# Decays of a delta rule: masked products and matmuls, or a row of running sums and a biased exp

## The chip, the cores and the metric

The program runs on 1 core of one Trainium2 chip. The core has a matrix engine (PE, with its weight loads PEld), a vector engine (DVE), a scalar engine (ACT), GpSimd (POOL) and DMA queues that its SyncE (SP), ACT and POOL issue to. The metric is the device time of one execution in microseconds, lower is better. Each engine runs its own instructions in a fixed order; an instruction that waits holds up all that stand behind it on the same engine or queue.

## The reference, cut to what matters

One residual layer over 1024 tokens of 1024 channels: a projection, two branches (a gated delta rule with 8 heads, and gated linear attention with 4), their output projections, gates and a norm. Both branches run forward and backward. The change touches the delta rule alone. For one head and one direction, within a chunk:

```python
g = jnp.cumsum(to_chunks(g), axis=-1)              # running sums of log decays
diff = g[..., :, None] - g[..., None, :]
decay = jnp.where(incl, jnp.exp(jnp.where(incl, diff, 0.0)), 0.0)
kb = k * beta[..., None]
lower = jnp.where(strict, jnp.einsum("bhnid,bhnjd->bhnij", kb, k) * decay, 0.0)
sol = lax.linalg.triangular_solve(lower, rhs, left_side=True, lower=True, unit_diagonal=True)
attn = jnp.einsum("bhnid,bhnjd->bhnij", q, k) * decay
v_new = u_n - w_n @ S
o = qd_n @ S + attn_n @ v_new
S = S * exp(gl_n) + kd_n^T @ v_new
```

The keys k are normalised to length one. The kernel works in chunks of 128 tokens, which gives the same result.

## The kernel before

The tokens lie in 8 chunks of 128. Channels are on the partitions, tokens on the free axis, except for keys and values by tokens (`ktok`, `vtok`). The program has these stages in order: the norm of x and its transposes; the gates of the scans (`scan_gates`, L407); eight heads of the delta rule; four heads of linear attention; two output projections; the merged output.

For each head h of the delta rule there are four pieces. `gdn_project` (L487) projects the keys, queries and values (`pj_a`) and the gate z (`pj_z`), convolves them on DVE (L506, L508) and applies SiLU on ACT (L489). `gdn_decay` (L573) makes `dt`, the decay from token j to token i for 16 units (8 chunks by 2 directions). `gdn_inverse` (L592) takes the norms of the keys (L608, into `n2`), the products of the keys (`pgr`, L624), multiplies them by `dt` and a factor c1 (beta over the squared norm) into `um` (L629), and inverts 1 + um: copies into `ul` on ACT (L636), blocks of 32 by substitution on DVE (L652, L654, 480 instructions each in all), blocks of 64 and 128 by matmuls (L683 to L722). Last it multiplies `dt` by the products of keys and queries (L741). `gdn_scan` (L744) runs over the chunks in 8 steps, both directions side by side: `psc` (L779) from the state, `r` on DVE (L781), `psc` (L784) with the inverse, `vd` on DVE (L787) and `vn` on ACT (L789), `psc` (L794) and the new state `S` on DVE (L799), and products into the output `po` (L768).

A scheduler orders each engine's instructions by places that the code gives: the inverse of head h comes first, then the decays of head h + 1 (`P_DT`), then the scan of head h (`P_Z`), which therefore lies beside the next head's inverse. Projections of the next head and, in the last head, 13 blocks of gates (`pj_t`) have the last place (`P_FILL`); their matmuls fill PE wherever nothing else is ready. The order is fixed when the program is built. `dt` has two buffers, so the decays of head h + 1 wait for the end of head h - 1's scan. The banks of `pacc` (tags o0, o1) serve `pd`, the matmuls of the decays, and `po` in turn.

Weights come through SP's queue into two raw buffers (`raw_a` and the like, L174), are cast on ACT into a high part (L177), and get their low part from POOL (L181) or DVE (L183). The row `qe` (L749) is a broadcast of one row of `eg_d` in DRAM to 128 partitions, on SP's queue.

Of the kernel before, what the change touches and what calls it, by code (L numbers as in the profile page):

```python
# [88 lines left out]
def layer_kernel(  # L89
# [200 lines left out]
    # ------------------------------------------------------------ constants of the two mixers  # L290
# [13 lines left out]
    strict_r = [mconst.tile([P, P], F32R, name=f"strict{d}") for d in range(2)]  # L304
    strict = [t.bitcast(F32) for t in strict_r]
# [14 lines left out]
    # ------------------------------------------------------------ h = rmsnorm(x), transposed  # L320
    with tc.tile_pool(name="xpool", bufs=2) as xpool:
        xt = [xpool.tile([P, D], F32, tag="xt", name=f"xt{t}", bufs=NT) for t in range(NT)]
        wpre = xpool.tile([P, D], F32, tag="wpre", name="wpre", bufs=1)
        stl = xpool.tile([P, 2, P], F32, tag="stl", name="stl", bufs=1)
# [20 lines left out]
        def scaled(t):  # L345
            """a tile of x normalised, its transpose"""
# [27 lines left out]
        nc.sync.dma_start(stl, consts[:, CONSTS["su"][0]:CONSTS["su"][0] + 2 * P].rearrange("p (d i) -> p d i", d=2))  # L374
# [9 lines left out]
        for d in range(2):  # L384
            nc.gpsimd.tensor_copy(strict_r[d], stl[:, d])
# [14 lines left out]
    # ------------------------------------------------------------ decays and gates of the scans  # L400
# [753 lines left out]
```

## Time and profile before

| what | value |
|---|---|
| time, median of 3 runs | 1592.54 us (1591.32 to 1592.92) |
| profiled execution: its span, the only time that the page gives of it | 1591.5 us |
| PE busy | 1526.6 us, 96% |
| PEld busy | 1283.3 us, 81% |
| DVE busy | 928.0 us, 58% |
| ACT busy | 673.1 us, 42% |
| POOL busy | 201.8 us, 13% |
| mean granted clock of PE, as a share of 2.4 GHz | 0.982 |

Busy time is the union of an engine's instructions. Matmuls overlap, so PE can be busy all the time and still not issue as fast as it can. The first products of the keys (L624) of the eight heads stand at 87.8, 172.4, 268.1, 357.2, 440.8, 531.4, 611.7 and 703.5 us, and the last scan ends at 797 us; from there to 900 us PE has the gate blocks that are left.

### The profile page before, as it was taken

The numbers are of one execution on the slowest core, as the hardware profiler recorded it, in microseconds if no ns is written. First come the engines' busy times: TensorE is split into PE (matmuls) and PEld (weight loads), VectorE is DVE, ScalarE is ACT, GpSimd is POOL, SyncE is SP. The second block draws the span as 40 slices with busy tenths as digits, with TensorE's granted clock in tenths as the row PEclk, the third lists the DMA queues.
The fourth block names the chain that finished last, engine by engine and source line by source line (L and its number), as shares of the span: only waits on it lengthen the run. The fifth ranks groups of instructions, "written<-read, shape, count | busy, mean of one in ns | idle before, by whom it ended". The sixth has DMA issues, their size and how long they took to land.

```text
span 1591.5 us, 25255 instructions
## 1 busy us (share of the span) xinstructions
PE 1526.6 (96%) x9622; PEld 1283.3 (81%) x9622; DVE 928.0 (58%) x2467; ACT 673.1 (42%) x1370; POOL 201.8 (13%) x225
## 2 busy tenths in 40 slices
PE   6998999999999999999999999999999999999998
PEld 6877787787878878787778898898888988787887
DVE  5497779979999899887511113314323355445413
ACT  5552535343444545453232325525436355433311
POOL 4242112111112121000000120110100100000000
PEclk9998999999999999998999999999999999999999
DMA  5221102121212121024143331231221335655404
GB/s 168 72 73 34 41 28 86 41 73 35 93 34 71 51 81 47 30 81 133 40 142 94 86 75 38 62 79 34 75 59 41 106 89 190 212 169 175 134 27 157
DMA packets 140882, 133.48 MB, mean 84 GB/s; under 512 B 11147, under 2 KB 114875, under 8 KB 140757
## 3 DMA queue, kind: packets, MB, share of 16 engines
q1 hardware_dynamic: 133282, 117.78, 25.0%
q10 hardware_dynamic: 6840, 12.00, 2.5%
q0 software_dynamic: 640, 2.10, 0.4%
q8 instruction: 75, 1.23, 0.3%
q14 instruction: 45, 0.37, 0.1%
HBM read 101.45 MB, written 30.39 MB: 83 GB/s over the span
## 4 chain that ended last, share of the span: by engine, by line
PE 62%; DVE 11%; DMA 6%; ACT 3%; issue 1%; SPq 1%; ACTq 0%; DVEq 0%
PE pj_t L251 9%; PE pj_y L251 7%; PE pj_v L240 6%; PE pout L141 5%; PE pj_a L251 5%; PE pj_g L251 5%; DVE tmp L652 3%; PE pj_q L251 3%; PE pj_k L251 3%; DVE yl L654 3%; PE pj_z L251 2%; PE po L768 2%; PE psb L946 2%; PE pob L968 2%; PE psc L794 1%; DMA st<-ob_d 1%
## 5 line engine op out<-in xcount | busy, mean ns | idle before, releaser
L251 PE MATMUL pj_a<-hh,hi_a 128*128 128x512 f32 x368 | 151.7, 412 | 0.0
L251 PE MATMUL pj_a<-hl,hi_a 128*128 128x512 f32 x368 | 151.0, 410 | 0.0
L251 PE MATMUL pj_a<-hh,lo_a 128*128 128x512 f32 x368 | 150.5, 409 | 0.0
L251 PE MATMUL pj_t<-hh,hi_t 128*128 128x512 f32 x256 | 103.9, 406 | 2.4 <-ACT gt L281 2.4
L251 PE MATMUL pj_t<-hh,lo_t 128*128 128x512 f32 x256 | 104.4, 408 | 0.0
L251 PE MATMUL pj_t<-hl,hi_t 128*128 128x512 f32 x256 | 104.3, 407 | 0.0
L181 POOL TENSOR_TENSOR lo_a<-raw_a,hi_a 128x512 fp32r<-128x512 f32 x48 | 68.6, 1430 | 235.1 <-ACT hi_a L177 224.9
L789 ACT ACTIVATE vn<-psc,c 128x128 f32<-128x128 f32 x128 | 45.0, 366 | 116.4 <-DVE vd L787 88.8
L652 DVE TENSOR_TENSOR tmp<-ulb,yl 128x54 f32<-128x54 f32 (+13 forms) x480 | 93.3, 235 | 1.3 <-DMA yl<-in_consts_dram 1.2
L654 DVE TENSOR_TENSOR yl<-yl,tmp 128x54 f32<-128x54 f32 (+13 forms) x480 | 90.9, 231 | 0.1
L251 PEld LDWEIGHTS pj_a<-hl,hi_a 128*128 128x128 f32 x368 | 71.1, 193 | 12.6 <-issue 1.0
L251 PEld LDWEIGHTS pj_a<-hh,lo_a 128*128 128x128 f32 x368 | 70.6, 192 | 12.8 <-issue 0.7
L251 PEld LDWEIGHTS pj_a<-hh,hi_a 128*128 128x128 f32 x368 | 70.6, 192 | 12.2 <-issue 0.7
L251 PE MATMUL pj_y<-ob,hi_y 128*128 128x512 f32 x256 | 79.1, 390 | 0.9 <-DVE gb L1073 0.9
L141 PE MATMUL pout<-wo,hh 128*128 128x512 f32 (+1 forms) x272 | 79.7, 377 | 0.0
L240 PE MATMUL pj_v<-lo_v,hh 128*128 128x256 f32 x256 | 72.4, 283 | 0.0
L240 PE MATMUL pj_v<-hi_v,hl 128*128 128x256 f32 x256 | 72.4, 283 | 0.0
L240 PE MATMUL pj_v<-hi_v,hh 128*128 128x256 f32 x256 | 72.4, 283 | 0.0
L181 POOL TENSOR_TENSOR lo_v<-raw_v,hi_v 128x512 fp32r<-128x512 f32 x32 | 41.3, 1290 | 231.9 <-ACT hi_v L177 226.1
L183 DVE TENSOR_TENSOR lo_t<-raw_t,hi_t 128x512 fp32r<-128x512 f32 x32 | 22.0, 689 | 64.1 <-ACT hi_t L177 64.0
L251 PEld LDWEIGHTS pj_t<-hh,hi_t 128*128 128x128 f32 x256 | 49.3, 193 | 12.2 <-ACT gt L281 2.8
L141 PEld LDWEIGHTS pout<-wo,hh 128*128 128x128 f32 x272 | 50.1, 188 | 9.4
(313 smaller groups left out, 4071.3 us busy)
## 6 DMA issues: line engine op xcount, KB each, us to landing
raw_a<-in_w_in_dram SPq DMA_DIRECT2D x48, 256.0 KB
qe<-eg_d SPq DMA_DIRECT2D x16, 512.0 KB
raw_t<-in_w_in_dram SPq DMA_DIRECT2D x32, 256.0 KB
gt_d<-gt SPq DMA_DIRECT2D x64, 128.0 KB
raw_v<-in_w_in_dram SPq DMA_DIRECT2D x32, 256.0 KB
xt<-in_x_dram SPq DMA_DIRECT2D x8, 512.0 KB
raw_z<-in_w_in_dram SPq DMA_DIRECT2D x16, 256.0 KB
z_d<-gz SPq DMA_DIRECT2D x32, 128.0 KB
```

Source lines behind the costliest of these rows:

```text
L141: nc.tensor.matmul(ps, lhsT=a(k), rhs=b(k), start=(s == 0), stop=(s == len(steps) - 1))
L181: nc.gpsimd.tensor_tensor(lo, raw, hi.bitcast(F32), op=ALU.subtract)
L183: nc.vector.tensor_tensor(lo, raw, hi.bitcast(F32), op=ALU.subtract)
L240: nc.tensor.matmul(ps[b][:, c * 256:(c + 1) * 256], lhsT=a[th][:, kk, ts], rhs=w[:, k, :], start=kk == 0 and i == 0 and c == 0, stop=kk == ...
L251: nc.tensor.matmul(ps[:, cols], lhsT=a[:, k, :], rhs=b[th][:, kk, cols], start=kk == 0 and a is hi and b is src[0], stop=kk == KD - 1 and ...
L652: nc.vector.tensor_tensor(tv, ul2[:, i, 0:i].unsqueeze(2).broadcast_to([P, i, w_]), yv[:, i].unsqueeze(1).broadcast_to([P, i, w_]), op=ALU ...
L654: nc.vector.tensor_tensor(yv[:, 0:i], yv[:, 0:i], tv, op=ALU.subtract)
L768: nc.tensor.matmul(po_n(n), lhsT=lhsT, rhs=rhs, start=count[b] == 1, stop=count[b] == len(todo[b]))
L789: nc.scalar.mul(vn[d], pc[d][:, P:2 * P], c1[:, d, n:n + 1])
L794: nc.tensor.matmul(pc[d][:, 2 * P:3 * P], lhsT=ktok[:, ns], rhs=vd[d], start=True, stop=True)
L946: nc.tensor.matmul(p_s[:, :256], lhsT=ktok[:, u], rhs=vt[:, n], start=True, stop=True)
L968: nc.tensor.matmul(po[e][:, j * P:(j + 1) * P], lhsT=a, rhs=b, start=(i == 0), stop=(i == len(todo) - 1))
```

## The change

`gdn_decay` no longer multiplies masks by log decays on DVE (`xm`, 16 instructions a head) and sums them with 16 float32r matmuls a head (`pd`), with an exp (four of 512 columns) and a select of the causal part (four on POOL) behind them. `scan_gates` now makes the running sums from the middle of each chunk for all heads at once, as two more small matmuls, transposes them and writes them to DRAM (`cr_d`, 16 small DMAs on SP's queue). `gdn_decay` then broadcasts a head's row of 2048 sums to all partitions with one DMA on SP's queue (1 MB in SBUF) and puts -1e30 at the places that are not causal with two selects on POOL. The exp moves into `gdn_inverse`: 16 instructions of 128 columns on ACT, each with a bias per partition that holds the negative running sum, the logarithm of beta and minus the logarithm of the squared norm of the key. So c1 is inside `dt`: `um` becomes four DVE products of 512 columns in place of 16 scaled ones of 128, and `vn` becomes a plain copy. The Ln of the squared norms (`nk`) moves from behind the inverse to in front of the exps. beta comes from exp and ln in place of a sigmoid.

```diff
+    cr_d = dram.tile([HA, 2, T], F32, name="cr_d")
...
+        mid = pool.tile([P, 2, 130], F32, tag="t2", name="mid", bufs=4)
+        nc.scalar.dma_start(mid, consts[:, o_c:o_c + 260].rearrange("p (d i) -> p d i", d=2))
...
-        nc.scalar.activation(be, ab[:, 2:4], AF.Sigmoid)
+        for o, v in ((sp, av), (lb, ab[:, 2:4])):
+            nc.scalar.activation(o, v, AF.Abs)
+            nc.scalar.activation(o, o, AF.Exp, scale=-1.0)
+            nc.scalar.activation(o, o, AF.Ln, bias=eps_t["one"][:, 0:1])
+        nc.vector.scalar_tensor_tensor(fl(lb), fl(ab[:, 2:4]), 0.0, fl(lb), op0=ALU.min, op1=ALU.subtract)
+        nc.scalar.activation(be, lb, AF.Exp)
...
+            o = 384 + d * 64
+            nc.tensor.matmul(psg[:, o:o + 64], lhsT=mid[:, d, :P], rhs=rhs, start=True, stop=True)
+        nc.vector.tensor_scalar(cm, psg[:, 384:512], 16.0, None, op0=ALU.mult)
+        nc.vector.tensor_tensor(fl(nb), fl(lb), cm, op=ALU.subtract)
+            nc.tensor.transpose(peg[:64, (2 + d) * P:(3 + d) * P], cm[:, d * 64:d * 64 + 64], ident)
+            for h in range(HA):
+                nc.sync.dma_start(cr_d[h, d].rearrange("(n i) -> n i", i=P), eg[h * NT:(h + 1) * NT, 2 + d])
...
     def gdn_decay(h, pool):
         dt = pool.tile([P, U, P], F32, tag="dt", name=f"dt{h}", bufs=2)
-        for d in range(2):
-            for g in range(2):
-                pd = bank(pacc, f"o{g}", f"pd{h}_{d}_{g}")
-                for j in range(2):
-                    ns = slice(4 * g + 2 * j, 4 * g + 2 * j + 2)
-                    for w_, src in enumerate((lgh.bitcast(F32), lgl)):
-                        m = pool.tile([P, 2, P], F32R, tag="xm", name=f"xm{h}_{d}_{g}_{j}_{w_}", bufs=2)
-                        nc.vector.tensor_tensor(m, mask[d].unsqueeze(1).broadcast_to([P, 2, P]),
-                                                src[:, d, h, ns].unsqueeze(2).broadcast_to([P, 2, P]), op=ALU.mult)
-                        nc.tensor.matmul(pd[:, 256 * j:256 * j + 256], lhsT=strict_r[d],
-                                         rhs=m.rearrange("p u i -> p (u i)"), start=w_ == 0, stop=w_ == 1)
-                us = slice(d * NT + 4 * g, d * NT + 4 * g + 4)
-                nc.scalar.activation(dt[:, us].rearrange("p u i -> p (u i)"), pd, AF.Exp)
-                causal(dt[:, us], dt[:, us], d, 4)
+        nc.sync.dma_start(dt.rearrange("p u i -> p (u i)"),
+                          cr_d[h:h + 1].rearrange("h d t -> h (d t)").broadcast_to([P, 2 * T]))
+        for d in range(2):
+            s = 1 - 2 * d
+            us = slice(d * NT, (d + 1) * NT)
+            nc.gpsimd.affine_select(dt[:, us], dt[:, us], pattern=[[0, NT], [s, P]], compare_op=ALU.is_ge,
+                                    fill=-1e30, base=0, channel_multiplier=-s)
         return dt
...
+        tc.keep_in_program_order(nc.scalar.activation(nk, n2, AF.Ln))
+        bias = sm.tile([P, 2, NT], F32, tag="bias", name=f"bias_{h}")
+        nc.vector.tensor_tensor(bias, nb[:, :, h], nk.unsqueeze(1).broadcast_to([P, 2, NT]), op=ALU.subtract)
+        for g in range(2):
+            for d in range(2):
+                for n in range(4 * g, 4 * g + 4):
+                    u = d * NT + n
+                    nc.scalar.activation(dt[:, u], dt[:, u], AF.Exp, bias=bias[:, d, n:n + 1])
...
-            for j in range(4):
-                n = 4 * g + j
-                for d in range(2):
-                    u = d * NT + n
-                    nc.vector.scalar_tensor_tensor(um[:, u], pk[:, j * P:(j + 1) * P], c1[:, d, n:n + 1], dt[:, u],
-                                                   op0=ALU.mult, op1=ALU.mult)
+            for d in range(2):
+                us = slice(d * NT + 4 * g, d * NT + 4 * g + 4)
+                nc.vector.tensor_tensor(um[:, us], by128(pk), dt[:, us], op=ALU.mult)
...
-                nc.scalar.mul(vn[d], pc[d][:, P:2 * P], c1[:, d, n:n + 1])
+                nc.scalar.copy(vn[d], pc[d][:, P:2 * P])
```

Lines of the changed file are a few off those of the old one: the SiLU is L499, the Ln L613, the exps L622, `um` L633, `ul` L639, `vn` L791.

On ACT, in the sixth head (number 5), this stood between the squares of the keys (`pk`) and the copies into `ul`:

```order
L608 ACTIVATE pk_1_6081,n_5_6070<-pk_1_6081 128x128
L789 ACTIVATE vn_1_4_5967<-psc_1_4_5952,c_4_5070 128x128
L789 ACTIVATE vn_0_5_5990<-psc_0_5_5979,c_4_5070 128x128
L489 ACTIVATE zs_5829<-zs_5829 128x1024
L310 ACT_TABLE_LOAD
L177 CAST hi_a_6_0_6601<-raw_a_6_0_6599 128x512
L636 COPY ul_6126<-um_6099 32x32x8 x4
L494 COPY xp_6_6564<-pj_a_6_0_6567 128x512
L789 ACTIVATE vn_1_5_5995<-psc_1_5_5980,c_4_5070 128x128
```

The same place of the changed kernel:

```order
L605 ACTIVATE pk_1_5816,n_5_5805<-pk_1_5816 128x128
L791 COPY vn_0_2_5641<-psc_0_2_5630 128x128
L791 COPY vn_1_2_5646<-psc_1_2_5631 128x128
L613 ACT_TABLE_LOAD
L613 ACTIVATE nk_5827<-n_5_5805 128x8
L499 ACT_TABLE_LOAD
L499 ACTIVATE zs_5564<-zs_5564 128x1024
L622 ACT_TABLE_LOAD
L622 ACTIVATE dt_5263<-dt_5263,bias_5833 128x128 x16
L639 COPY ul_5868<-um_5853 32x32x8 x4
L791 COPY vn_0_3_5669<-psc_0_3_5658 128x128
L791 COPY vn_1_3_5674<-psc_1_3_5659 128x128
```

The Ln, the exps and two more table loads now stand between the squares and `ul`, and the next `vn` of the scan stands behind them. In the whole order ACT has 57 table loads where it had 38.

On DVE, this stood at the start of head 3's scan, where head 4's decays were made (`xm` are the masked products, `vd`, `S` and `r` the scan's own, `v` a convolution of the next head):

```order
L583 TENSOR_TENSOR xm_1_1_0_0_4497<-call,lgh 128x256
L787 TENSOR_SCALAR vd_1_0_4830<-psc_1_0_4823,c_3_4046 128x128
L583 TENSOR_TENSOR xm_1_1_0_1_4500<-call,lgl 128x256
L583 TENSOR_TENSOR xm_1_1_1_0_4503<-call,lgh 128x256
L797 COPY S_0_0_4835<-psc_0_0_4822 128x128
L583 TENSOR_TENSOR xm_1_1_1_1_4506<-call,lgl 128x256
L583 TENSOR_TENSOR xm_0_0_0_0_5477<-call,lgh 128x256
L797 COPY S_1_0_4838<-psc_1_0_4823 128x128
```

And at the start of head 3's scan in the changed kernel:

```order
L789 TENSOR_SCALAR vd_0_0_4607<-psc_0_0_4604,c_3_3875 128x128
L789 TENSOR_SCALAR vd_1_0_4612<-psc_1_0_4605,c_3_3875 128x128
L518 SCALAR_TENSOR_TENSOR v_4295<-xp_4_4440,cw,v_4295 128x1024
L799 COPY S_0_0_4617<-psc_0_0_4604 128x128
L799 COPY S_1_0_4620<-psc_1_0_4605 128x128
L518 SCALAR_TENSOR_TENSOR v_4295<-xp_4_4440,cw,v_4295 128x1024
```

The scan's steps no longer have masked products between them; convolutions that stood later move up.

On SP's queue, this stood behind the gates of the scans, before the first head:

```order
L459 DMA eg_d<-scr 64x128 x2
L749 DMA qe_0_1737<-eg_d 128x1024
L174 DMA raw_a_1_0_829<-in_w_in_dram 128x4x128
L749 DMA qe_0_1740<-eg_d 128x1024
L174 DMA raw_a_1_1_872<-in_w_in_dram 128x4x128
```

The same place of the changed kernel:

```order
L467 DMA eg_d<-eg 64x128
L469 DMA cr_d<-eg 8x128 x8
L467 DMA eg_d<-eg 64x128
L469 DMA cr_d<-eg 8x128 x8
L175 DMA raw_a_1_0_799<-in_w_in_dram 128x4x128
L580 DMA dt_620<-cr_d 128x2048
L580 DMA dt_1351<-cr_d 128x2048
L751 DMA qe_0_1660<-eg_d 128x1024
L751 DMA qe_0_1663<-eg_d 128x1024
L175 DMA raw_a_1_1_842<-in_w_in_dram 128x4x128
```

The second half of the second head's first weights (`raw_a_1_1`) now stands behind four broadcasts, and these behind 18 small writes.

## Rows read from the trace of the kernel before

**Rows 1.** Page, part 1: busy us, share of the span, instructions.

```profile
PE 1526.6 (96%) x9622; PEld 1283.3 (81%) x9622; DVE 928.0 (58%) x2467; ACT 673.1 (42%) x1370; POOL 201.8 (13%) x225
```

**Rows 2.** Busy time by stage: us, then busy us and instructions of each engine, granted clock.

```profile
core 0: us, PE busy (x) PEld busy (x) DVE busy (x) ACT busy (x) POOL busy (x), PEclk, DMA share, GB/s
0.00:100.00 100.00, 84.37 (x513) 74.11 (x513) 62.64 (x107) 59.94 (x112) 36.95 (x44) 0.98 0.37 109
100.00:268.00 168.00, 156.74 (x1156) 127.61 (x1154) 141.10 (x434) 67.02 (x150) 33.08 (x39) 0.95 0.17 51
268.00:804.00 536.00, 512.02 (x3864) 425.78 (x3865) 458.82 (x1478) 243.22 (x524) 79.19 (x96) 0.97 0.21 64
804.00:1282.00 478.00, 474.43 (x2678) 406.90 (x2677) 127.56 (x219) 190.02 (x369) 52.55 (x46) 1.00 0.26 72
```

**Rows 3.** Chain that ended last, 268 to 804 us: shares by line.

```profile
by line: PE pj_a L251 15.7%; DVE tmp L652 8.6%; DVE yl L654 7.9%; PE pj_z L251 6.7%; PE po L768 5.4%; PE pj_t L251 4.4%; PE psc L794 3.3%; PE psc L784 2.9%; DVE xm L583 2.9%; PE psc L779 2.8%; PE p L710 2.4%; PE p L718 2.3%; PE pgr L624 2.2
```

**Rows 4.** Groups of instructions by line: count | busy us, mean ns | idle before, releasers.

```profile
L585 PE MATMUL pd<-xm,strict 128*128 128x256 f32 x128 | 38.8, 325 | 10.2 <-DVE xm L583 8.5 <-DVE o L465 1.0
L583 DVE TENSOR_TENSOR xm<-call,lgl 128x256 fp32r<-128x256 f32 x64 | 33.7, 527 | 0.3 <-PE pd L585 0.3
L583 DVE TENSOR_TENSOR xm<-call,lgh 128x256 fp32r<-128x256 f32 x64 | 32.1, 502 | 10.8 <-PE pd L585 10.2
L629 DVE SCALAR_TENSOR_TENSOR um<-pgr,c,dt 128x128 f32<-128x128 f32 x128 | 33.8, 343 | 1.0 <-PE pgr L624 0.9
L741 DVE TENSOR_TENSOR dt<-pkq,dt 128x512 f32<-128x512 f32 x32 | 19.8, 681 | 2.2 <-PE pkq L738 2.2
L570 POOL TENSOR_SCALAR_AFFINE_SELECT dt<-dt 128x512 f32<-128x512 f32 x32 | 30.8, 963 | 104.0 <-ACT dt L588 94.0 <-PE pj_z L251 3.5 <-PE psc L794 3.4
L789 ACT ACTIVATE vn<-psc,c 128x128 f32<-128x128 f32 x128 | 45.0, 366 | 116.4 <-DVE vd L787 88.8 <-PE psc L784 17.4 <-DVE tmp L652 5.9
```

**Rows 5.** Long pieces of the chain, whole span: start us, us, what.

```profile
330.05 4.33 DMA qe<-eg_d
...
824.59 75.35 PE pj_t L251 x324
...
922.82 23.03 PE pj_v L240 x192
```

**Rows 6.** Waits of PE and PEld, 268 to 804 us: total us, times, longest.

```profile
PE psc L794 <- ACT vn L789: 9.4, 7, 2.2
...
PEld psc L794 <- ACT vn L789: 18.5, 29, 2.6
```

**Rows 7.** ACT in order of time, 531 to 540 us (head 5): start, us, what.

```profile
531.37 0.19 ACT L608 ACTIVATION_READ_ACCUMULATOR pk<-pk 128x1 f32 x1
531.46 0.62 ACT L789 ACTIVATE vn<-psc,c 128x128 f32<-128x128 f32 x2
531.96 1.06 ACT L489 ACTIVATE zs<-zs 128x1024 f32<-128x1024 f32 x1
533.04 1.28 ACT L310 ACT_TABLE_LOAD   x1
535.28 0.62 ACT L177 CAST hi_a<-raw_a 128x512 fp32r<-128x512 f32 x1 [0.96 <-issue]
536.60 2.65 ACT L636 COPY ul<-um 32x256 f32<-32x256 f32 x4 [0.70 <-DVE um L629]
```

**Rows 8.** ACT in order of time, 49 to 52 us.

```profile
49.64 1.28 ACT L310 ACT_TABLE_LOAD   x1
50.94 0.62 ACT L177 CAST hi_a<-raw_a 128x512 fp32r<-128x512 f32 x1
51.46 0.31 ACT L434 ACTIVATE scr<-scr 128x128 f32<-128x128 f32 x1
51.67 0.20 ACT L438 ACTIVATE scr<-scr 128x16 f32<-128x16 f32 x1
```

**Rows 9.** SP's queue in order of time, near the start.

```profile
62.34 1.15 SPq L459 DMA_DIRECT2D eg_d<-scr  x2
```

**Rows 10.** DVE in order of time, first head.

```profile
93.30 4.22 DVE L629 SCALAR_TENSOR_TENSOR um<-pgr,c,dt 128x128 f32<-128x128 f32 x16
```

More of the change, by code (lines that the diff above doesn't have):

```diff
@@ L303, in layer_kernel @@
     mask = (cst("iu"), cst("il"))
-    strict_r = [mconst.tile([P, P], F32R, name=f"strict{d}") for d in range(2)]
-    strict = [t.bitcast(F32) for t in strict_r]
     oi, _ = CONSTS["iu"]
@@ L323, in layer_kernel @@
         wpre = xpool.tile([P, D], F32, tag="wpre", name="wpre", bufs=1)
-        stl = xpool.tile([P, 2, P], F32, tag="stl", name="stl", bufs=1)
         cwn = xpool.tile([5, 3 * D], F32, name="cwn", tag="cwn", bufs=1)
@@ L373, in layer_kernel @@
         nc.sync.dma_start(cwn, conv_w)
-        nc.sync.dma_start(stl, consts[:, CONSTS["su"][0]:CONSTS["su"][0] + 2 * P].rearrange("p (d i) -> p d i", d=2))
         nc.sync.dma_start(gdn_w, gdn_norm_w.rearrange("a p -> p a"))
@@ L383, in layer_kernel @@
         halves_of(NT - 1)
-        for d in range(2):
-            nc.gpsimd.tensor_copy(strict_r[d], stl[:, d])
         ps_sm = [pacc.tile([64, 512], F32, tag=f"o{th}", name=f"pj_sm_{th}") for th in range(2)]
@@ L402, in layer_kernel @@
     be = mconst.tile(SC, F32, name="be")
-    lgh = mconst.tile(SC, F32R, name="lgh")
-    lgl = mconst.tile(SC, F32, name="lgl")
+    nb = mconst.tile(SC, F32, name="nb")
     ev = mconst.tile([P, 2, 3, HA, NT], F32, name="ev")
@@ L416, in scan_gates @@
         smT = pool.tile([64, T], F32, tag="osq", name="smT", bufs=1)
+        stl = pool.tile([P, 2, P], F32, tag="stl", name="stl", bufs=1)
+        nc.scalar.dma_start(stl, consts[:, CONSTS["su"][0]:CONSTS["su"][0] + 2 * P].rearrange("p (d i) -> p d i", d=2))
+        mid = pool.tile([P, 2, 130], F32, tag="t2", name="mid", bufs=4)
+        nc.scalar.dma_start(mid, consts[:, o_c:o_c + 260].rearrange("p (d i) -> p d i", d=2))
+        strict = [stl[:, d] for d in range(2)]
         ones = part(tb_, 3, 1)
@@ L433, in scan_gates @@
         sp = v4(part(tb_, 1, 1))
-        nc.scalar.activation(sp, av, AF.Abs)
-        nc.scalar.activation(sp, sp, AF.Exp, scale=-1.0)
-        nc.scalar.activation(sp, sp, AF.Ln, bias=eps_t["one"][:, 0:1])
+        lb = v4(part(tc_, 1, 1))
+        for o, v in ((sp, av), (lb, ab[:, 2:4])):
+            nc.scalar.activation(o, v, AF.Abs)
+            nc.scalar.activation(o, o, AF.Exp, scale=-1.0)
+            nc.scalar.activation(o, o, AF.Ln, bias=eps_t["one"][:, 0:1])
         nc.vector.scalar_tensor_tensor(fl(sp), fl(av), 0.0, fl(sp), op0=ALU.max, op1=ALU.add)
+        nc.vector.scalar_tensor_tensor(fl(lb), fl(ab[:, 2:4]), 0.0, fl(lb), op0=ALU.min, op1=ALU.subtract)
+        nc.scalar.activation(be, lb, AF.Exp)
         nc.scalar.activation(alog, alog, AF.Exp)
@@ L441, in scan_gates @@
         nc.vector.tensor_scalar(lg, lg, -1.0, None, op0=ALU.mult)
-        nc.vector.tensor_copy(lgh, lg)
-        nc.vector.tensor_tensor(lgl, lg, lgh.bitcast(F32), op=ALU.subtract)
         psg = bank(pg, "g", "psg")
@@ L450, in scan_gates @@
                 nc.tensor.matmul(psg[:, o:o + 64], lhsT=m, rhs=rhs, start=True, stop=True)
+            o = 384 + d * 64
+            nc.tensor.matmul(psg[:, o:o + 64], lhsT=mid[:, d, :P], rhs=rhs, start=True, stop=True)
         nc.scalar.activation(ev, psg[:, :384].rearrange("p (d q h n) -> p d q h n", d=2, q=3, h=HA), AF.Exp)
         nc.vector.tensor_scalar(nE, ev[:, :, 0], -1.0, None, op0=ALU.mult)
+        cm = part(ta_, 0, 1)
+        nc.vector.tensor_scalar(cm, psg[:, 384:512], 16.0, None, op0=ALU.mult)
+        nc.vector.tensor_tensor(fl(nb), fl(lb), cm, op=ALU.subtract)
         peg = bank(pg, "g", "peg")
@@ L455, in scan_gates @@
             nc.tensor.transpose(peg[:64, d * P:(d + 1) * P], ev[:, d, 0].rearrange("p h n -> p (h n)"), ident)
-        eg = part(ta_, 2, 2)[0:64].rearrange("p (d i) -> p d i", d=2)
-        nc.vector.tensor_copy(eg.rearrange("p d i -> p (d i)"), peg[:64, :2 * P])
+            nc.tensor.transpose(peg[:64, (2 + d) * P:(3 + d) * P], cm[:, d * 64:d * 64 + 64], ident)
+        eg = pool.tile([64, 4, P], F32, tag="t2", name="eg", bufs=4)
+        nc.vector.tensor_copy(eg.rearrange("p d i -> p (d i)"), peg[:64])
         for d in range(2):
             nc.sync.dma_start(eg_d[d].rearrange("h (n i) -> (h n) i", i=P), eg[:, d])
+            for h in range(HA):
+                nc.sync.dma_start(cr_d[h, d].rearrange("(n i) -> n i", i=P), eg[h * NT:(h + 1) * NT, 2 + d])
     def finish(o_ps, wcol, rs, zs, o, dst, kc):
@@ L722, in gdn_inverse @@
             (nc.vector.tensor_copy, nc.scalar.copy)[d](um[a, us_of[d], e], p3[a].rearrange("p (n i) -> p n i", i=64))
-        tc.keep_in_program_order(nc.scalar.activation(nk, n2, AF.Ln))
-        nc.scalar.activation(nk, nk, AF.Exp, scale=0.5)
+        tc.keep_in_program_order(nc.scalar.activation(nk, nk, AF.Exp, scale=0.5))
         for g in range(2):
@@ L741, in gdn_inverse, with gdn_scan @@
                 nc.vector.tensor_tensor(dt[:, us], by128(pk), dt[:, us], op=ALU.mult)
-        return dt, um, ktok, vtok, c1, c2
-    def gdn_scan(h, pool, sm, qkv, dt, um, ktok, vtok, c1, c2):
+        return dt, um, ktok, vtok, c2
+    def gdn_scan(h, pool, sm, qkv, dt, um, ktok, vtok, c2):
         qT, kT, _ = qkv
```

4 lines of the change are left out of this document (removed).

## The prediction

> **What bounds the kernel now.** I read the page's busy times first: PE is busy 96% of the span, DVE 58%, ACT 42%, POOL 13% [rows 1]. That makes PE the bound on average and says nothing of single stages, so the windows by stage come next [rows 2]. The reader is to see two different regimes. From 804 to 1282 us PE is busy 474 of 478 us at a granted clock of 1.00; nothing of the change lies there. From 268 to 804 us, where the delta rule of the heads runs among projections, PE is busy 512 of 536 us, but DVE is at 459 too, and the clock is 0.97. There the chain that ended last is read by line [rows 3]: it goes to and fro between PE (projections, state products) and DVE (`tmp`, `yl`, `xm`); the masked products `xm` have 2.9% of it, 15.5 of 536 us. So both engines set the time in that stage, PE more than DVE. Last come the groups of instructions for prices [rows 4], the waits of the scan [rows 6], and ACT in order of time around one head [rows 7], since the change puts its new work on ACT.
>
> **What goes from PE.** 128 matmuls `pd` go, 16 a head. Their rows say 325 ns each [rows 4], but that is a latency in a pipeline; what a 256-column matmul of the same kind of operand takes when nothing stops it is read from a long stretch of projections, 23.03 us for 192 [rows 5], 0.120 us each. So 128 x 0.120 = 15.4 us of work. The same group had PE idle for 10.2 us ahead of it, 8.5 by `xm`; these go with it. Together -25.6 us. What could take the idle time back is the next wait in line, below.
>
> **What goes from DVE.** The `xm` products have 33.7 + 32.1 = 65.8 us. `um` had 128 instructions and 33.8 us; four products of 128 x 512 a head are 32 in all, and the like product at L741 took 19.8 us for 32 [rows 4]. So DVE loses 65.8 + 14.0 = 80 us. I do not count these again: most of it stood beside PE's work, and the part for which PE waited is already in the 10.2 us. If DVE's share of the chain came through in full, that is rival B.
>
> **What POOL does.** Four selects of 512 columns a head become two of 1024. At 963 ns for one of 512 the total is 30.8 us before [rows 4] and between 15.4 (cost by instruction) and 30.8 us (by column) after, on an engine that is busy 13%. Nothing; the select waits for a broadcast issued a head earlier, and that cover lasts tens of microseconds.
>
> **What comes to ACT, and who waits for it.** Between the squares of a head's keys and the copies `ul`, ACT had two `vn`, the SiLU `zs`, a table load and a cast [rows 7]: the squares end at 531.56, `ul` ends at 539.25, 7.7 us. In the changed order this stretch holds two `vn` (0.62), a load (1.28), the Ln (of 8 columns, about 0.2 by the small one in [rows 8]), a load, `zs` (1.06), a load, 16 exps with a bias, and `ul` behind the last `um` (0.62 + 2.65). An exp of 128 columns with a bias per partition is not in the trace. From below, an activation of 128 columns issues 0.21 us before the next (51.46 to 51.67) [rows 8]; from above, one `vn` with a scale per partition has a mean of 366 ns [rows 4], and two together take 0.62 [rows 7]. I take 0.30, near the pair of `vn`, which has the same sort of operand: 4.8 us. The sum is 0.62 + 1.28 + 0.2 + 1.28 + 1.06 + 1.28 + 4.8 + 0.62 + 2.65 = 13.8 us, so 6.1 us more than before. In all ACT gets 19 loads more, 24 us, and loses four exps of 512 columns a head; at 42% busy it has the room, the order is what counts.
>
> Queued behind this block on ACT stand the next `vn` of the previous head's scan; DVE's `S` and the next state products wait for those. Before, in 268 to 804 us PE and its loads waited for `vn` for 9.4 + 18.5 = 27.9 us [rows 6], and the places lie among seven heads' scans that have such a block in them (the eighth has none behind it): 4.0 us each at a block of 7.7. Grown in proportion, 6.1/7.7 of 4.0 is 3.2 us a head. Part of this is covered: in the changed order 34 projection matmuls stand ahead of the state product of head 4 that needs the `vn` behind head 5's block, 34 x 75.35/324 = 7.9 us [rows 5]. Not all heads have so many, so I take half, 1.6 us a head, 11 us in all. The bounds are 0 (cover everywhere) and 7 x 6.1 = 43 us (none).
>
> The Trainium skill, page "ScalarE: Activation LUTs", section "What ACT_TABLE_LOAD costs", speaks against the change here: a switch of tables is said to cost a drain of about 1380 ns besides the load's 1283 ns. In this trace the load takes 1.28 us, as the page says, and the next instruction starts 0.02 us after it [rows 8]; what stands ahead of it, 0.02 us too at 533.04, shows no gap either [rows 7]. By the page, as an estimate, the block would grow by two drains, 2.8 us; I take the trace.
>
> **The start.** After the gates SP issued two writes in 1.15 us, 0.58 each [rows 9]. Now 18 stand there, 16 more or 9.2 us, then two broadcasts of 1 MB and the two `qe`. A `qe` of 512 KB took 4.33 us [rows 5], so 1 MB takes between 4.3 (issue-bound) and 8.7 us (by bytes). From 62.3, the first head's row is there by about 62.3 + 10.4 + 8.7 = 81.4, its exps (two selects of at most 1.9, 16 x 0.30 and two loads of 1.28) by 93; `um` began at 93.30 and ended at 97.5 [rows 10], and will take 2.5 instead of 4.2. So it just fits. Late is the second half of head 1's weights, queued behind all this, and with it ACT's cast that stands before the exps. Bounds 0 and 9.2 + 4.8 = 14 us (neither issues nor exps covered); I take 5, a third, because the 31 us from the gates to `um` hold most of it. Later broadcasts are issued behind the previous scan, a head ahead of their use; if that cover were missing, 8.7 us a head.
>
> **Sum.** -25.6 + 11 + 5 = -9.6 us on the span of 1591.5, the only time the page gives of its execution. The median of the runs, 1592.5, lies 1.0 above it, so the forecast is 1591.5 - 9.6 + 1.0 = 1583 us. Its own range follows from its unknown terms: both additions at zero give 1567, and at 11 + 11 us they give 1589.
>
> **Rivals.**
> - B, DVE was the true limit between 100 and 804 us. For it: DVE at 459 of 536 us and `xm` on the chain. Against it: PE at 512. Then PE's 15.4 us go, and the 15.5 us of `xm` on the chain, which are those of five heads, become 24.8 for eight; ACT's block is covered. 1592.5 - 15.4 - 24.8 + 5 = 1557.
> - C, slower: ACT's block stalls the scan. The next `vn` waits behind Ln, three loads and 16 exps; `S` and the state products wait for it, and `um` for the exps, with the scan's own DVE steps queued behind `um`. For it: the waits for `vn` are already the scan's largest [rows 6]. Against it: the projections that stand between. It decides from the point at which the uncovered delay is over (25.6 - 5)/7 = 2.9 us a head; the block gives at most 6.1. Half way between, 4.5 a head is 31.5: 1592.5 - 25.6 + 31.5 + 5 = 1603.5.
> - C', a drain at every load. By two in each of seven blocks, what the load itself takes is the nearest row, 1.28: 14 x 1.28 = 18 us more than C's half-way case, 1621. No gap in [rows 8] bears it out; the page of the Trainium skill named above has such a rule.
> - D, nothing is gained: `pd` and `xm` were fillers in the scan's gaps, and PE now waits there instead. For it: PE's waits for `vn` [rows 6]. Against it: `pd` had waits of its own. Then -25.6 is eaten by waits as long as the work that left, and the time is 1592.5, within 3 us.
>
> **How the numbers follow.** Chances: forecast 0.44, B 0.16, C 0.22, C' 0.03, D 0.15. A measurement of this kernel can tell about 0.2%, 3.2 us, from no change. Forecast and B are faster, 0.60; D is the same, 0.15; C and C' slower, 0.25. The range goes from B's 1557 to 1608, C with 5.1 us a head; what lies beyond, half of B's far side, C above that and C', is not over 0.2.
>
> **What the profile after would show.** Right: `pd` and `xm` gone, PE with about 128 matmuls less, DVE's busy time down by some 80 us, `um` 32 times at about 0.62 us, ACT's block from the squares to `ul` near 14 us, exps 0.2 to 0.37 us apart, and waits of the scan for `vn` grown by some 11 us. The first `um` should end at 95 to 105 us. B is right if PE's idle time shrinks beyond the 10 us of `pd`; C if state products wait for `vn` or `S` by more than 3 us a head; D if PE's idle time has grown by what its work shrank; C' if a gap over 1 us stands by each load. The forecast is wrong if the broadcasts land after their selects could start, if the first scan begins over 14 us late, or if the clock in 268 to 804 us leaves 0.97 by more than 0.01, which no term here covers.

## The result, and the profile after

The changed kernel takes 1644.84 us (median, 1644.12 to 1647.96) where the kernel before took 1591.93 beside it: a ratio of 1.0344, 95% interval 1.0317 to 1.0372. It is some 54 us slower; 1583 were forecast. The profiled execution spans 1646.2 us, 54.7 more than before.

The page's busy times of the kernel after, and its windows by stage (columns as in [rows 1, 2]):

```profile
PE 1538.3 (93%) x9500; PEld 1295.8 (79%) x9500; DVE 871.7 (53%) x2252; ACT 704.3 (43%) x1488; POOL 190.5 (12%) x207
```

```profile
0.00:100.00 100.00, 79.30 (x476) 69.74 (x476) 54.36 (x72) 57.71 (x118) 30.56 (x40) 0.96 0.40 124
100.00:268.00 168.00, 142.56 (x925) 118.20 (x926) 117.87 (x367) 60.18 (x134) 27.88 (x34) 0.84 0.20 59
268.00:804.00 536.00, 498.24 (x3786) 415.80 (x3785) 412.31 (x1311) 269.38 (x617) 78.47 (x85) 0.95 0.21 65
804.00:1282.00 478.00, 464.43 (x2554) 393.82 (x2553) 135.40 (x253) 182.50 (x366) 45.80 (x42) 0.99 0.27 73
```

PE has 122 instructions fewer and yet is busy longer, 1538.3 against 1526.6 us [rows 1]. It is also idle longer: 1646.2 - 1538.3 = 107.9 us against 64.9. The granted clock is lower where PE idles more: 0.84 in 100 to 268 us where before had 0.95, 0.95 against 0.97 in 268 to 804 [rows 2]. The two levels are 1.2 and 2.4 GHz, so a mean of 0.84 is a third of that stretch at the lower one.

The trace tells how much of the loss is idle time and how much is slower matmuls. Summed over the stretches in which the granted clock is 0.50, PE is busy for 118.0 us, where before has 54.6. The 63.4 us more would have been half at the upper level: an estimate of 31.7 us lost. So the 54.7 us are 43.0 of idle time and 31.7 of slower matmuls, less some 20 of work that did leave PE.

What ACT does around the sixth head, after (columns as in [rows 7], which shows the same place before):

```profile
562.58 0.19 ACT L605 ACTIVATION_READ_ACCUMULATOR pk<-pk 128x1 f32 x1
562.66 0.42 ACT L791 COPY vn<-psc 128x128 f32<-128x128 f32 x2
563.11 1.28 ACT L613 ACT_TABLE_LOAD   x1
564.40 0.21 ACT L613 ACTIVATE nk<-n 128x8 f32<-128x8 f32 x1
564.63 1.28 ACT L499 ACT_TABLE_LOAD   x1
565.92 1.06 ACT L499 ACTIVATE zs<-zs 128x1024 f32<-128x1024 f32 x1
566.98 1.28 ACT L622 ACT_TABLE_LOAD   x1
568.28 4.79 ACT L622 ACTIVATE dt<-dt,bias 128x128 f32<-128x128 f32 x16
572.97 2.57 ACT L639 COPY ul<-um 32x256 f32<-32x256 f32 x4
575.57 0.43 ACT L791 COPY vn<-psc 128x128 f32<-128x128 f32 x2
```

From the squares' end at 562.77 to the end of `ul` at 575.54 are 12.8 us; 13.8 were worked out, 7.7 were there before. No gap of a drain stands by a load (564.39 to 564.40, 568.26 to 568.28), so the loads cost 1.28 us each and rival C' is out. (The prediction passed over one line of [rows 7]: behind the load at 533.04 a cast starts 0.96 us late, with nothing shown that it waited for. Casts have such gaps without a load ahead too, 1.89 us at 196.93 in the kernel after, so it need not be a drain; 53 of the 57 loads in the kernel after have the next instruction within 0.05 us.)

On PE, two of the four long stops from 80 to 804 us show what was not foreseen:

```profile
95.34 0.39 PE L252 MATMUL pj_z<-hh,lo_z 128*128 128x512 f32 x1
102.83 0.79 PE L252 MATMUL pj_a<-hh,hi_a 128*128 128x512 f32 x1 [7.10 <-ACT gz L282]
...
210.67 0.39 PE L252 MATMUL pj_a<-hl,hi_a 128*128 128x512 f32 x1
210.90 0.39 PE L252 MATMUL pj_a<-hh,lo_a 128*128 128x512 f32 x1
219.96 0.80 PE L252 MATMUL pj_a<-hh,hi_a 128*128 128x512 f32 x1 [8.67 <-ACT xp L504]
220.55 0.63 PE L252 MATMUL pj_a<-hl,hi_a 128*128 128x512 f32 x1
220.98 0.63 PE L252 MATMUL pj_a<-hh,lo_a 128*128 128x512 f32 x1
```

And on ACT at the first of them, then at the second:

```profile
94.40 4.79 ACT L622 ACTIVATE dt<-dt,bias 128x128 f32<-128x128 f32 x16
99.09 2.50 ACT L639 COPY ul<-um 32x256 f32<-32x256 f32 x4
101.61 0.62 ACT L178 CAST hi_a<-raw_a 128x512 fp32r<-128x512 f32 x1
102.14 0.64 ACT L282 COPY gz<-pj_z 128x256 f32<-128x256 f32 x2
...
210.29 4.78 ACT L622 ACTIVATE dt<-dt,bias 128x128 f32<-128x128 f32 x16
214.98 2.50 ACT L639 COPY ul<-um 32x256 f32<-32x256 f32 x4
217.50 1.28 ACT L309 ACT_TABLE_LOAD   x1
218.80 0.62 ACT L178 CAST hi_a<-raw_a 128x512 fp32r<-128x512 f32 x1
219.32 1.06 ACT L504 COPY xp<-pj_a 128x512 f32<-128x512 f32 x2
```

The reader is to see that the filling itself stops. A projection's results leave PSUM through a copy on ACT (`gz`, `xp`), and that copy stands behind the exps and `ul`. PE, in its fixed order, stands still until that copy is done. After the stop the matmuls come 0.43 us apart (220.55 to 220.98) where they came 0.23 us apart before it (210.67 to 210.90); the granted clock is 0.50 from 215.0 to 225.2 us. The other two stops, of 6.2 and 7.4 us, end with a result of DVE in the inverse (`xq`), for which the next matmul in PE's order waits. A group of before and those of the kernel after, with the columns of [rows 4]:

```profile
L251 PE MATMUL pj_a<-hh,hi_a 128*128 128x512 f32 x368 | 151.7, 412 | 0.0
...
L252 PE MATMUL pj_a<-hh,hi_a 128*128 128x512 f32 x368 | 153.6, 417 | 16.5 <-ACT xp L504 9.4 <-ACT gz L282 7.1
...
L622 ACT ACTIVATE dt<-dt,bias 128x128 f32<-128x128 f32 x128 | 38.3, 388 | 0.4 <-DVE bias L615 0.3
...
L585 POOL TENSOR_SCALAR_AFFINE_SELECT dt<-dt 128x1024 f32<-128x1024 f32 x16 | 25.9, 1646 | 30.3 <-DMA dt<-cr_d 30.2
...
L633 DVE TENSOR_TENSOR um<-pgr,dt 128x512 f32<-128x512 f32 x32 | 22.1, 691 | 27.7 <-ACT dt L622 24.5 <-PE pj_z L252 3.1
```

Waits of the kernel after, with the columns of [rows 6], for `vn` from 268 to 804 us; then PE's for `xq` from 80 to 804 us, before and after:

```profile
PEld psc L796 <- ACT vn L791: 33.4, 26, 3.8
...
PE psc L796 <- ACT vn L791: 23.8, 15, 3.4
...
PE p L683 <- DVE xq L662: 3.2, 2, 2.7
...
PE p L686 <- DVE xq L665: 19.0, 6, 7.4
```

Before, this group of `pj_a` has 0.0 us of idle time ahead of it; now it has 16.5. The scan's waits for `vn` are 33.4 + 23.8 = 57.2 us where they were 27.9 [rows 6]. The wait for the inverse grew from 3.2 to 19.0 us, about as much as that for the copies. The selects on POOL waited 30.2 us for their broadcasts, but the exps behind them waited 0.4 us in all, most of it for `bias`: the broadcasts held up nothing here.

The first products of the keys of the eight heads now stand at 87.5, 205.3, 289.0, 380.0, 472.7, 562.5, 655.6 and 739.6 us. Against before the second head is 33 us late. The third is 21 us late, so a part is made up, and from there the lateness grows again, to 44 us in the seventh head and 36 in the last. In the order on PE the first scan has moved: before, 17 projection matmuls after that scan's start the second head's inverse began beside it; now the whole scan stands ahead of that inverse.

### The profile page after: what moved, and what is told of

The parts are those of the page before. It is cut to its first block, busy times and chain, and to the rows that moved or that the text cites. A ratio compares the mean times of both kernels' runs of the same rounds, so it can differ in the third digit from the quotient of the medians.

```text
span 1646.2 us, 24982 instructions
## 1 busy us (share of the span) xinstructions
PE 1538.3 (93%) x9500; PEld 1295.8 (79%) x9500; DVE 871.7 (53%) x2252; ACT 704.3 (43%) x1488; POOL 190.5 (12%) x207
## 3 DMA queue, kind: packets, MB, share of 16 engines
q1 hardware_dynamic: 134546, 126.11, 25.6%
## 4 chain that ended last, share of the span: by engine, by line
PE 64%; DVE 16%; ACT 11%; DMA 5%; issue 3%; SPq 0%; POOL 0%; ACTq 0%; DVEq 0%; POOLq 0%
PE pj_t L252 8%; PE pj_y L252 7%; PE pj_v L241 6%; PE pout L141 5%; PE pj_g L252 5%; DVE yl L657 4%; PE pj_a L252 4%; DVE tmp L655 4%; PE pj_z L252 4%; PE pj_k L252 3%; PE pj_q L252 2%; ACT dt L622 2%; PE po L770 2%; PE psb L948 2%; PE pob L970 2%
## 5 line engine op out<-in xcount | busy, mean ns | idle before, releaser
L252 PE MATMUL pj_a<-hh,hi_a 128*128 128x512 f32 x368 | 153.6, 417 | 16.5 <-ACT xp L504 9.4
L182 POOL TENSOR_TENSOR lo_a<-raw_a,hi_a 128x512 fp32r<-128x512 f32 x48 | 63.8, 1329 | 311.0 <-ACT hi_a L178 257.0
L657 DVE TENSOR_TENSOR yl<-yl,tmp 128x54 f32<-128x54 f32 (+13 forms) x480 | 96.3, 241 | 0.1
L791 ACT COPY vn<-psc 128x128 f32<-128x128 f32 x128 | 32.2, 265 | 108.5 <-DVE vd L789 72.1
L796 PE MATMUL psc<-vd,ktok 128*128 128x128 f32 x224 | 45.4, 304 | 24.8 <-ACT vn L791 24.7
L796 PEld LDWEIGHTS psc<-vd,ktok 128*128 128x128 f32 x224 | 34.7, 198 | 39.5 <-ACT vn L791 37.7
```

What stands on the lines that cost most here:

```text
L182: nc.gpsimd.tensor_tensor(lo, raw, hi.bitcast(F32), op=ALU.subtract)
L252: nc.tensor.matmul(ps[:, cols], lhsT=a[:, k, :], rhs=b[th][:, kk, cols], start=kk == 0 and a is hi and b is src[0], stop=kk == KD - 1 and ...
L657: nc.vector.tensor_tensor(yv[:, 0:i], yv[:, 0:i], tv, op=ALU.subtract)
L791: nc.scalar.copy(vn[d], pc[d][:, P:2 * P])
L796: nc.tensor.matmul(pc[d][:, 2 * P:3 * P], lhsT=ktok[:, ns], rhs=vd[d], start=True, stop=True)
```

## Experiments

Each ratio is against the kernel before, run beside it; 0.1% are 1.6 us. The theories: **removal** (what left PE and DVE gains nothing), **block** (ACT's Ln, loads and exps hold up the path), **order** (the first scan stands alone), **start**. The differences below join runs by these ratios. Each edit has the scheduler build the whole order anew, so a difference between two runs can hold a part that is due to the order alone.

**x1, exps back at the decays' place.**

```
-  bias = nb - ln(norm); exps in gdn_inverse
+  exps in gdn_decay, bias=nb (minus the running sum); c1 back on um and vn
```

> The changed kernel with the 16 exps moved back to the decays' place (bias: minus the running sum alone), the Ln behind the inverse, and c1 back on um and vn. No Ln, no exps and no extra table loads stand between the squares and ul; but in the order scan 0 starts after 452 projection matmuls, as in the changed kernel (454; before 528). Theory block (ACT's Ln, loads and exps in front of each um cost the time, some 5 us a head and more): at or under the kernel before, 1575 to 1592. Theory order (scan 0 stands ahead of head 1's projections and runs alone, um of head 1 is 34 us late): the lateness of head 1 stays, 1615 to 1635.

1605.54 us, ratio 1.0108 (1.0072 to 1.0144). Neither: 2.4% come back, though the scan still stands alone. The second head's keys are later than in the changed kernel (211.1 us), but the last head's stand at 712.0, 8.5 us late: here the lateness is made up.

**x2, Ln behind the explicit load.**

```
+  tc.add_manual_dep(ln.ins, last_table[0].ins.name, NoSync)
```

> The changed kernel with one edge more: the Ln of the key norms is issued behind the explicit load of the exp and ln table, so a head has one load in its block and not three (37 loads in all where the changed kernel has 57), and in the new order scan 0 starts after 506 projection matmuls and lies beside the inverse of head 1. Theory block: two loads of 1.28 us less a head, about 20 us: 1625. Theory order: the 34 us of head 1 come back besides: 1590 to 1605.

1617.52 us, 1.0164 (1.0112 to 1.0216): loads and order changed together here, so x6 below tells the loads apart.

**x3, head 1's projections ahead of scan 0.**

```
-  with at(P_FILL + P_HEAD * (h + 1)):
+  with at(P_FILL + P_HEAD * (h + 1) if h else P_HEAD * (h + 1) + P_Z - 500):
```

> The changed kernel with the projections of head 1 placed ahead of scan 0 in the scheduler's order (scan 0 after 528 projection matmuls, as before); the ACT block with its loads is unchanged (54 loads). Theory order: um of head 1 near 180 us where it was 208, time 1610 to 1620. Theory block: no change, 1640 to 1650.

1619.27 us, 1.0194 (1.0160 to 1.0228). The order at head 0 is worth 1.5%, 24 us, with the ACT block in place. The lateness of the keys is 7 us in the second head and grows to 24 in the last.

**x4, two writes in place of 16.**

```
-  for h in range(HA): nc.sync.dma_start(cr_d[h, d]..., eg[h * NT:(h + 1) * NT, 2 + d])
+  nc.sync.dma_start(cr_d[d].rearrange("h (n i) -> (h n) i", i=P), eg[:64, 2 + d])
```

> The changed kernel with cr_d laid out by direction first, so that 2 writes replace the 16 small ones on SP's queue; the order of PE is nearly the same (scan 0 after 456). Theory start (the 16 writes make head 1 late): 5 to 15 us faster, 1630 to 1640. Theories order and block: within 3 us of the changed kernel, 1642 to 1648.

1645.62 us, 1.0362 (1.0314 to 1.0410): no gain. The writes are not what makes head 1 late.

**x5, x1 and x3 together.**

> Both edits at once: the exps at the decays' place without the key norm (x1) and the projections of head 1 ahead of scan 0 (x3). Scan 0 starts after 528 projection matmuls, 41 table loads. If block and order are two causes that add: 1645 - 40 - 25 = 1580, faster than the kernel before by 5 to 10 us. If they are one cause seen twice: as x1, about 1605.

1610.14 us, 1.0115 (1.0076 to 1.0153), as x1. The two do not add: where ACT's block is gone, the placing gains nothing.

**x6, x2 and x3 together.**

> The Ln behind the explicit table load (37 loads) together with the projections of head 1 ahead of scan 0. Against x3 (54 loads, 1619 us) only the loads in the block differ. If the loads cost their own 1.28 us each on the path, two a head: 1619 - 7 x 2.6 = 1601. If they are covered: 1617 to 1621.

1612.91 us, 1.0143 (1.0108 to 1.0177), 0.5% or 8 us under x3. The loads may cost something, under half of the full price that was expected; the intervals overlap, so it isn't told from nothing.

**x9, the exps alone in the inverse.** x5 with the 16 exps between the squares and `um`, without a Ln.

> As x5, but the 16 exps of a head stand in the inverse between the squares and um (a bias that is read with the norms, without a Ln): exps alone are moved, the Ln and its table loads are not there (43 loads). Theory block: 16 x 0.30 = 4.8 us a head come on the path of seven heads, up to 34 us over x5, half of it likely: 1590 to 1615. If only the loads and the Ln matter: as x5 within 5 us.

1611.99 us, 1.0142 (1.0103 to 1.0181). Over x5 by 4 us, inside the intervals: where the exps stand matters little.

**x7, useless work on DVE.**

```
+  if h == 0:
+      with at(P_HEAD * (h + 1) + P_DT):
+          for j in range(48): nc.vector.tensor_tensor(m, mask..., um..., op=ALU.mult)
```

> The changed kernel with 48 useless products of 128x256 on DVE in head 0, some 20 us of DVE work whose result nothing reads, at the place of the next head's decays. In the new order scan 0 starts after 481 projection matmuls and lies beside the inverse of head 1 (in the changed kernel it stands alone). Theory order: faster than the changed kernel, 1615 to 1635, though work was added. Theory that DVE work costs: 1645 to 1665.

1626.38 us, 1.0231 (1.0182 to 1.0279): work was added and 18 us came back. In the order 481 projection matmuls stand ahead of the scan in place of 454, and the second head's keys come at 192.6 us in place of 205.3. The scan lies beside the second inverse only in part: of its 88 `psc` matmuls 64 still stand ahead of it (all 88 in the changed kernel, 10 before).

**x12, only the removal.**

```
-  xm products, pd matmuls; exp(pd)
+  exp of the constant mask
```

> The kernel before with only the removal: the products xm on DVE and the matmuls pd on PE are gone, and the exp reads a constant mask in their place (the decays are left out of the computation). No broadcast, no Ln, no exps in the inverse. In the order scan 0 starts after 484 projection matmuls and stands alone, as in the changed kernel. My forecast's first term: 25 us faster than before, about 1565. Theory that the removal itself does harm (PE is short of other work, idles and its clock falls, and scan 0 stands alone): 1590 to 1610, with more than 85 us at half clock where before has 59.

1598.23 us, 1.0068 (1.0028 to 1.0109). This kernel leaves the decays' values out, as x15 and z4 do. Without 66 us of DVE work and 128 matmuls, and with nothing added, it is 0.7% slower; its first scan stands alone, with 484 projection matmuls ahead of it.

**x15, the removal with x3's placing.**

> As the run that leaves out xm and pd, with the projections of head 1 placed ahead of scan 0 (scan 0 after 528 matmuls, beside the inverse of head 1). If the order at head 0 is all the harm of the removal: 1565 to 1580, faster than before. If the idle PE and its lower clock are: within 6 us of the run without the placing.

1587.94 us, 0.9991 (0.9971 to 1.0010). The order is the 0.8% between x12 and x15; with it mended the removal gains nothing that can be told. Its windows show what became of the 15.4 us of PE:

```profile
100.00:268.00 168.00, 155.11 (x1153) 128.91 (x1152) 132.13 (x398) 71.34 (x157) 31.51 (x38) 0.94 0.19 56
268.00:804.00 536.00, 505.14 (x3777) 419.62 (x3776) 422.83 (x1378) 245.26 (x526) 75.91 (x94) 0.96 0.21 65
```

Against [rows 2] PE is idle for 1.6 + 6.9 us more. At the lower level of the clock it is busy there for 55.7 us where before has 47.8, an estimate of 4 us lost. That is 12.5 of the 15.4. The executions of the kernel before that were taken beside it lie up to 14 us apart, so an account from one profile of each can't be closer.

**x10 and x14, work like the removed put back as dead work**, on x1 and on x5.

```
+  nc.vector.tensor_tensor(m, mask..., nb..., op=ALU.mult)
+  nc.tensor.matmul(pd..., lhsT=hh..., rhs=m)      # nothing reads pd
```

> x1 (exps at the decays' place) with the removed work put back as dead work: 16 products xm a head on DVE and 16 matmuls pd a head on PE, whose result nothing reads; scan 0 starts after 474 matmuls and still stands alone. If the removed work was only load: x1 plus 15 to 25 us, 1620 to 1630. If PE's matmuls between the scan's steps kept its clock up: no slower than x1 (1605), with fewer than 95 us at half clock where x1 has 104.

> x5 (exps at the decays' place, head 1's projections ahead of scan 0) with the dead xm and pd put back. If the broadcast row, the selects, the 16 exps and the start cost nothing beside the kernel before, and removal is the harm: 1585 to 1595, faster than x5 (1610) though it has more work. If those additions cost: 1610 to 1630.

1634.75 us, 1.0289 (1.0255 to 1.0323), and 1613.55 us, 1.0173 (1.0133 to 1.0214). In the profiled executions the time at the lower clock does shrink with them, from 102.0 us in x1 to 87.5, and from 99.7 in x5 to 86.6, but neither is faster for it: x10 is 29 us slower than x1, x14 is 9 us slower than x5 with intervals that overlap. So the theory that the matmuls were useful as mere load falls. And what this work costs is no constant: 1 us between x15 and the kernel before, 9 and 29 here.

**z1, x3 with the copies of the gate z on DVE.**

```
-  nc.scalar.copy(g_, ps[...])
+  (nc.vector.tensor_copy if name[0] == "z" else nc.scalar.copy)(g_, ps[...])
```

> x3 (the changed kernel with head 1's projections ahead of scan 0; full ACT block) with the copies of the gate z out of PSUM (gz) on DVE in place of ACT. Theory evacuation (ACT's block holds up the copies that free PE's projection banks, so the filling stops too): x3's waits of pj_a for gz, 8.3 us of PE, go and the clock with them: 1600 to 1612 against x3's 1619. Theory that only vn matters: within 5 us of x3.

1602.43 us, 1.0083 (1.0051 to 1.0116), 18 us under x3, by moving a copy and with the order that was built with it: the second inverse begins right behind 528 projection matmuls, in x3 behind 557. The waits of PE from 80 to 804 us, of x3 and then of z1:

```profile
PE psc L796 <- ACT vn L791: 23.7, 13, 5.1
...
PE pj_a L252 <- ACT gz L282: 8.3, 2, 7.6
```

```profile
PE psc L796 <- ACT vn L791: 17.4, 11, 4.2
...
PE pj_a L252 <- ACT xp L504: 1.1, 1, 1.1
```

The wait for `gz` is gone, and of that for `vn` a quarter: the copies left ACT's queue. The two are 14.6 us less, but PE's waits for `xq` and `r` of DVE are 9.9 us more (9.6 + 4.3 in x3, 14.1 + 9.7 here), so what the order gives is not parted from it.

**z3, x5 with four exps of 512 columns.**

```
-  for n in range(NT): nc.scalar.activation(dt[:, u], dt[:, u], AF.Exp, bias=nb...)
+  for g in range(2): nc.scalar.activation(dt[:, u4], dt[:, u4], AF.Exp, scale=0.001)
```

> x5 with four exps of 512 columns a head without a bias in place of 16 of 128 with one (the running sum of the partition and so the decay's value is left out of the computation). ACT saves 2.4 us a head. Theory that the 16 exps are what is left: 1590 to 1600. Theory start: within 6 us of x5, 1604 to 1616.

1591.24 us, 1.0011 (0.9987 to 1.0036), 1.0% or 17 us under x5. This kernel leaves the running sum of the partition out. The trace shows a good part of the gain at the start: in x5 twelve exps, 3.62 us, and a SiLU with two table loads stand on ACT ahead of the first head's squares, and its keys' products come at 96.1 us; here one long exp, 0.63 us, stands there, and they come at 88.6. In the last head it is 715.9 against 698.0.

**z4, x15 with the changed kernel's start.**

> The run that leaves out xm and pd with head 1's projections placed first (x15, 1588), with the changed kernel's start: its gates, two more small matmuls, beta by exp and ln, the transposes and 16 writes; but no broadcast (the exp reads the constant mask). If the start is the 20 us between x15 and x5: 1600 to 1612. If the broadcast row and the 16 exps are: within 4 us of 1588.

1594.83 us, 1.0029 (1.0009 to 1.0048): over x15 by 6 us for the gates, transposes and writes at the start; the intervals just touch.

**z2, x5 with two writes and `gz` on DVE.**

> x5 (exps at the decays' place, no key norm in the bias, head 1's projections ahead of scan 0) with two writes in place of 16 and gz on DVE. If evacuation and the start are what is left of x5's lateness: 1585 to 1598, level with the kernel before. If not: 1605 to 1612.

1647.82 us, 1.0367 (1.0327 to 1.0406): a miss. The two edits that did no harm apart, on other kernels, gave here another order, in which the sixth head's inverse begins after the scan ahead of it, and PE waits for `vn` 33.3 us from 100 to 900 us. Whether the order does it was not tried further.

**w3, x5 with the running sum added on DVE**, four exps a head, and the first head's `gz` on DVE (that line is not shown below).

```
+  nc.vector.tensor_tensor(dt[:, u4], dt[:, u4], nb[...].unsqueeze(2).broadcast_to([P, 4, P]), op=ALU.add)
+  nc.scalar.activation(dt[:, u4], dt[:, u4], AF.Exp)      # four a head, no bias
```

> x5 with the running sum of the partition added on DVE (four sums of 128x512 a head, DVE has room) and four exps of 512 columns without a bias in place of 16 with one, and the copies of the first head's gate z out of PSUM on DVE; the whole reference is computed. Theory that the 16 exps and the held-up copies were the rest of x5's lateness: 1582 to 1594, level with the kernel before or a little under. Theory that DVE's four sums cost what the exps did: 1600 to 1612.

1593.42 us, 1.0023 (1.0001 to 1.0046). With the whole reference computed, the broadcast row comes within 4 us of the kernel before; no run makes a gain of it.

**w5, w3's sums without x3's placing, all `gz` on DVE.**

> x1 (no placing by hand of head 1's projections) with the sums on DVE and four exps, and all copies of the gate z on DVE; in its order scan 0 starts after 463 projection matmuls and lies beside the inverse of head 1. If the relief of ACT is what counts and the order is good: 1575 to 1592. If the order of the scheduler decides again (as in z2): over 1605.

1610.64 us, 1.0149 (1.0117 to 1.0181). In 720 to 804 us its PE is busy 67.7 of 84 us where w3's is 76.6: less load on ACT does not help in that order. There too 76 of the first scan's 88 `psc` matmuls stand ahead of the second inverse.

## Why the prediction was wrong

By the ratios the loss stacks up, from the kernel before to the changed one: removal with a good order (x15) -1 us, the start (z4) +6, the broadcast with 16 exps a head (x5) +14, the exps, Ln and loads in front of `um` (x3) +13, the first scan alone (the changed kernel) +24. The sum is 55 (unrounded). This is one path of several, and the steps do not add in another: by way of x1, ACT's block is worth 38 us and the first scan nothing.

- **"Together -25.6 us" failed.** The count was right: 122 PE instructions fewer on the page (the gates added some). DVE is at 871.7, down 56 where 80 were forecast; `xm` and `um` gave 77 of these (65.8 + 33.8 - 22.1), and what took 21 back is open. But x15 shows -1 us. In its order the work was filler in a stage in which PE waits for chains: without it idle time and a lower clock stand in its place. Rival D named this for the whole change, with 0.15; for this term, in that order, it was the case. Put back on x1 the same sort of work cost 29 us, so the term is one of the order and not of the work alone.
- **"In the changed order 34 projection matmuls stand ahead" failed most.** I priced ACT's block by who waits for `vn` and let projections cover it. They need ACT too: their banks are emptied by `gz` and `xp` behind the same block, and PE waited 16.5 us for these. That wait had no row before, since it was zero, and I listed only `vn` as queued behind the block. The term itself was short too: the waits for `vn` grew by 29.3 us where 11 were taken, 4.2 a head, which is over rival C's mark of 3. Rival C had the block, its size (12.8 us measured) and the sign, but not the copies; its 1603.5 (its terms add up to 1603.4) was 41 us short.
- **The exps were taken at 4.8 us a head, and measured 4.79.** I counted them only as part of the block. In x5 they stand elsewhere, and z3 still gives 17 us back for four long ones in place of 16: an engine at 42% busy was not free where they stood ahead of the first head's squares (96.1 against 88.6 us). It isn't the copies here: PE's wait for `gz` is 6.3 us in x5 and 7.4 in z3. Where the rest of the 17 us comes from is not shown.
- **The order had no term.** I read the orders of ACT, DVE and SP for who stands behind whom, and not on PE where scan 0 stands. Without `xm` on DVE the first scan comes earlier in the order (x12 shows it for the removal alone), with 454 projection matmuls ahead of it in place of 528; the second head's keys aren't ready, and the scan runs alone. Then the second inverse runs alone too: from 208 to 290 us PE is busy 65.91 of 82 us, where before had 91.23 of 96 at the like place (174 to 270 us; the first line).

```profile
174.00:270.00 96.00, 91.23 (x692) 75.26 (x691) 84.76 (x262) 41.41 (x93) 16.20 (x20) 0.98 0.17 53
...
100.00:208.00 108.00, 98.65 (x651) 82.30 (x652) 67.48 (x211) 37.08 (x88) 17.61 (x20) 0.85 0.19 57
208.00:290.00 82.00, 65.91 (x468) 54.60 (x467) 57.67 (x172) 39.96 (x85) 13.32 (x17) 0.83 0.20 58
```

- **The start was right in its number, by luck in part:** +5 taken, 6 measured (z4). It was argued from 16 writes (9.2 us) that make head 1's weights late and from exps that aren't covered. The writes took 2.83 + 2.84 = 5.7 us, two in their place gained nothing (x4), and z4 has neither the broadcasts nor the exps. What in the start costs the 6 us was not tried. Head 0's last `um` ended at 99.9, inside 95 to 105.
- **The forecast's own test, a clock that leaves 0.97 by more than 0.01, came true** (0.95), and "no term covers it" was the right warning: by the estimate above slower matmuls cost 31.7 us. Rival B is out by its own sign, since PE's idle time grew by 43.0 us and did not shrink.

Open: why x1 makes up its lateness and the changed kernel doesn't, so that the same placing gains 24 us there and nothing on x1; and what in z2's order costs.

## What to carry over

Before work is taken off an engine, ask what the next limit of that stage is; in a stage of chains with filler, the work that leaves may be filler too (x15), or may not (x10). When an engine gets a longer block, list everything that is queued behind it, the copies that empty PSUM first: their wait reads zero until the day it doesn't. And where a scheduler builds the order, compare on the bound engine where whole stages stand, since a faster piece can start a stage before its companion is ready.

## What was not expected of the hardware

The lower clock level outlives the wait: it stood until 225.2 us, 5 us past the end of the 8.67 us stop, and the same matmuls came 0.43 us apart where they had come 0.23 apart. So that stop cost more than its length. A stop is not all that goes with it: before, PE was busy for 54.6 of the 56.6 us at the lower level, and what brought it on there no run shows.

As forecast, but dear for its size: 16 biased exps of 128 columns took 4.79 us where four of 512 without a bias had 0.60 each (2.4 us), before:

```profile
91.66 0.60 ACT L588 ACTIVATE dt<-pd 128x512 f32<-128x512 f32 x1 [1.19 <-PE pd L585]
```
